# q and both gates of two blocks by Strassen's algorithm, in a stage of their own ahead of the mixers

## The chip, the cores and the metric

The kernel runs on one NeuronCore of a Trainium2 chip. The metric is the device time of one execution in microseconds (us). The core has five engines that run their own instruction streams in order and wait for one another by semaphores: TensorE (PE), VectorE (DVE), ScalarE (ACT), GpSimd (POOL) and SyncE (SP). Here SP only issues DMA transfers; POOL and ACT issue some as well. A static scheduler has fixed the order of the instructions on every engine before the program runs.

## The reference

One layer of a hybrid decoder in one inference step: 2048 prompt tokens (4 blocks of 512 for the kernel) and 32 sample tokens, width 1024, feed-forward width 4096.

```python
h = _rmsnorm(x, n1)
z = h @ w_in
hq, hf, hi, hg, sq, sk, sv, ga, gb = jnp.split(z, np.cumsum(IN_SPLITS)[:-1], axis=-1)
f = lb + (1.0 - lb) * jax.nn.sigmoid(hf)
o_hg, s_new = _hgrn_recurrence(heads(hq), heads(jnp.log(f)), heads(1.0 - f), heads(hi), s0, chunk)
y_a = (_rmsnorm(o_hg, hg_norm_w) * jax.nn.silu(hg)) @ w_up_a
y_b = o_b @ w_up_b                       # o_b: sliding-window attention of sq, sk, sv
m = jax.nn.sigmoid(ga) * y_a + jax.nn.sigmoid(gb) * y_b
x = x + m @ w_o
h2 = _rmsnorm(x, n2)
x = x + jnp.square(jax.nn.relu(h2 @ w_ff1)) @ w_ff2
```

hq has 512 columns, gb and ga have 1024 each. Everything is float32.

## The kernel before

**Precision.** A float32 operand is split into a high and a low part (`split_out`, L229: ACT rounds the high part with a cast, DVE subtracts it to get the low one). A product is then three matmuls into the same bank: high x high, high x low, low x high. So a product of 1024 rows by a tile of 128 columns and 512 tokens takes 8 x 3 = 24 matmuls of 512 columns.

**Order of the stages.** The loop over the blocks (L318) takes the four blocks b0 to b3 of 512 tokens; b3 carries the 32 sample tokens too (544 tokens, in two segments of 288 and 256 columns). A block goes through the mixers: hi (`colN512`, L391), four heads of hq (`colT`, L356), sq (`colN512`), skv (`colN`, L383), sliding-window attention (swa) with the heads of hf as filler, the levels of the HGRN recurrence (lv) with hg as filler, the outputs of the recurrence, then gate b, gate a, and W_o. After an odd block follows the MLP for the pair of blocks, f1 and f2, both by Strassen's algorithm (7 products for 8, classes Wpair and Unit, L971 and L1008) with the two blocks as halves of the token dimension. The pair b0, b1 has one chunk of 512 columns in it, the pair b2, b3 two of 264.

**The gates** (`gate`, L777): for each of 8 tiles j of 128 columns, 24 matmuls into a mm bank (gbb or gab in the trace: h times w_in), a tanh on ACT (sigmoid(x) = 0.5 tanh(x/2) + 0.5), 12 matmuls into a sw bank (ybb or yab: times W_up), and a DVE operation that joins them (L788). In gate a, POOL adds gate b's result pb (L813) and the sum is split into mT, W_o's operand. After every second j of the first two blocks, the program calls `w2_sums` (L302) once: 4 loads, 4 DVE sums, 4 stores that prepare the Strassen operands of W2 in DRAM.

**Operands and buffers.** The normalized, transposed input of a block lies split in SBUF (hT, two large slots of eight). It is made tile by tile (`load_T_parts`, L251): square on ACT, power on POOL (`rstd_of`, L197), scaling, 8 transposes on PE, products with the norm's weights on DVE, split. Block 0's tiles stand at the program's start, the tiles of b1 and b3 in W_o of the block before, those of b2 in f2 of the first pair (L1195). Weights are read in tiles of 128 x 1024 from a ring of 12 buffers (`wtile`, L73), loaded by SP and split (`split_w`, L148). The last operation of f2, in the first pair, is Fin (L1137): output rows are transposed back (fy), added to x (fx), squared, powered (fr) and scaled. The accumulators yacc of f2 lie in a pool that is freed after it.

Of the kernel before, what the change touches and what calls it, by code (L numbers as in the profile page):

```python
# [16 lines left out]
P = 128  # L17
# [26 lines left out]
def tile_hybrid_step(  # L44
# [188 lines left out]

    def geometry(bi):
# [16 lines left out]
    def load_T_parts(bi, i, hT, xt, on_dve=False, sm=None, junk=None, hwf=None):  # L251
        kind, r0, nr, c = geometry(bi)[5][i]
        src = xs if kind == "s" else xp[bi * bt + c * P:bi * bt + (c + 1) * P, :]
        N = f"ab{bi}{c}"
        x = []

        def pre():
            x.append(xt())
            nc.sync.dma_start(x[0][0:nr, :], src)
            norm_pre(x[0], x[0], nr, N, on_dve, sm, junk and junk())  # L260

        def out(half, tp, wb):
            hw = (hwf or t2)(f"hw_{N}_{half}")[:, 0:512].rearrange("p (k t) -> p k t", k=4)[:, :, 0:nr]
            nc.vector.tensor_tensor(hw, tp, wb, ALU.mult)
            split_out(hT[half][:, 0, :, r0:r0 + nr], hT[half][:, 1, :, r0:r0 + nr], hw)

        return pre, lambda: norm_post(x[0], nr, n1c, N, out)

    wk_ctx = ExitStack()
    wk = wk_ctx.enter_context(tc.tile_pool(name="wk0", bufs=1, reuse_waits="tile"))  # L270
    hT_next = start_T(0)
    x_first = op(6, F32, "x_first")
    for i in range(ncb):
        for part in load_T_parts(0, i, hT_next, lambda: x_first[:, i * D:(i + 1) * D], on_dve=True):
            part()
# [43 lines left out]
    for bi in range(nblk):  # L319
# [16 lines left out]
        hT_cur = hT_next  # L336
        h_acts = [(hT_cur[k // 4][:, 0, k % 4, :], hT_cur[k // 4][:, 1, k % 4, :]) for k in range(KD)]

        n4 = 4 * bt
        W0 = op(2, F32, "W0_" + B)  # L340
        W1 = op(3, F32, "W1_" + B)
        qW = W0[:, 0:n4].rearrange("p (h t) -> p h t", h=HH)
        kW = W0[:, n4:2 * n4].rearrange("p (h t) -> p h t", h=HH)
        fW = W1[:, 0:n4].rearrange("p (h t) -> p h t", h=HH)
        aW = W1[:, n4:2 * n4].rearrange("p (h t) -> p h t", h=HH)
        aflat = W1[:, n4:2 * n4]
# [6 lines left out]
        if smp:  # L353
            vS = wk.tile([NS, 512], F32, tag="vS", name="vS")
# [122 lines left out]
        while late:  # L477
            norm_post(*late.pop(0))
# [484 lines left out]
        with tc.tile_pool(name=f"f1_{sb}", bufs=1, reuse_waits="tile") as fp:  # L963
# [115 lines left out]
            for i, u in enumerate(units):  # L1079
                if i % len(chunks) == 0:  # L1080
                    u.pair.rest()
                if i >= ahead:
                    u.a()
# [262 lines left out]
```

## Time and profile before

| | |
|---|---|
| median of 3 runs | 2930.8 us (2928.26 to 2934.26) |
| the profiled execution | 2930.84 us |
| its span in the trace | 2929.1 us |
| mean granted TensorE clock | 0.992 |
| instructions of TensorE | 19967 matmuls and as many weight loads |
| bytes moved by DMA | 443.9 MB, mean 152 GB/s |

The page of the profile says for each engine how long it was busy and with how many instructions. A timeline row is a start, a duration, the engine, the line of the kernel, and the operation as out<-in. A windows row gives busy times by engine in a stretch of the span, with the granted clock and the DMA's share and rate. Stages of the first pair in the trace: the first transposes start at 10.6 us and hi at 18.2, gates b and a of block 0 run from 216 to 342, W_o to 390, block 1 to 758, f1 to 1078, f2 to 1399. The second pair ends at 2929.

### The profile page before, as it was taken

The numbers are of one execution on the slowest core, as the hardware profiler recorded it, in microseconds if no ns is written. First come the engines' busy times: TensorE is split into PE (matmuls) and PEld (weight loads), VectorE is DVE, ScalarE is ACT, GpSimd is POOL, SyncE is SP. The second block draws the span as 40 slices with busy tenths as digits, with TensorE's granted clock in tenths as the row PEclk, the third lists the DMA queues.
The fourth block names the chain that finished last, engine by engine and source line by source line (L and its number), as shares of the span: only waits on it lengthen the run. The fifth ranks groups of instructions, "written<-read, shape, count | busy, mean of one in ns | idle before, by whom it ended". The sixth has DMA issues, their size and how long they took to land.

```text
span 2929.1 us, 49035 instructions
## 1 busy us (share of the span) xinstructions
PE 2841.5 (97%) x19967; PEld 2453.5 (84%) x19967; DVE 1629.4 (56%) x2559; ACT 1136.1 (39%) x2093; POOL 215.0 (7%) x360
## 2 busy tenths in 40 slices
PE   7999999999899999999999999999998999999998
PEld 6778877788778888887777888878997999999998
DVE  5674434734777674454456343275347777754446
ACT  3443334423433344442354233333234333344433
POOL 0110111101200000000111011100003000000001
PEclk9999999999999999999999999999999999999999
DMA  7746342145654465565422434212346454485553
GB/s 251 238 154 219 105 144 66 45 122 158 197 165 155 159 232 206 196 214 173 151 64 68 125 115 135 62 52 84 116 133 197 151 157 140 146 304 179 186 195 104
DMA packets 410539, 443.92 MB, mean 152 GB/s; under 512 B 22588, under 2 KB 290840, under 8 KB 410296
## 3 DMA queue, kind: packets, MB, share of 16 engines
q1 hardware_dynamic: 402160, 413.48, 44.0%
q0 software_dynamic: 5600, 18.70, 2.1%
q10 hardware_dynamic: 2552, 8.60, 0.8%
q8 instruction: 157, 2.57, 0.4%
q14 instruction: 70, 0.57, 0.1%
HBM read 334.07 MB, written 107.64 MB: 151 GB/s over the span
## 4 chain that ended last, share of the span: by engine, by line
PE 43%; DMA 3%; DVE 2%; ACT 1%; issue 1%; POOL 1%; SPq 0%; POOLq 0%; DVEq 0%; ACTq 0%
PE f L1180 3%; PE f L1179 3%; PE f L1181 3%; PE fB L959 2%; PE fB L961 2%; PE fB L960 2%; PE gab L169 1%; PE gab L170 1%; PE gab L168 1%; PE gbb L170 1%; PE gbb L169 1%; PE gbb L168 1%; PE fD L959 1%; PE fD L961 1%; PE fD L960 1%
## 5 line engine op out<-in xcount | busy, mean ns | idle before, releaser
L1179 PE MATMUL f<-f2S,hw2T 128*128 128x264 f32 (+1 forms) x576 | 183.7, 319 | 0.0
L1180 PE MATMUL f<-f2S,hw2T 128*128 128x264 f32 (+1 forms) x576 | 183.6, 319 | 0.0
L1181 PE MATMUL f<-f2S,lw2T 128*128 128x264 f32 (+1 forms) x576 | 183.5, 319 | 0.0
L155 DVE TENSOR_TENSOR lw2T<-lw2T,hw2T 128x1024 fp32r<-128x1024 f32 x64 | 78.1, 1224 | 106.0 <-ACT hw2T L154 105.5
L959 PE MATMUL fB<-S,w1T 128*128 128x264 f32 (+1 forms) x384 | 124.2, 325 | 7.3 <-DVE c L1027 3.7
L1180 PE MATMUL f<-f2A,h_w2B 128*128 128x264 f32 (+1 forms) x384 | 122.5, 319 | 1.4 <-DVE f2A L155 1.4
L961 PE MATMUL fB<-S,w1T 128*128 128x264 f32 (+1 forms) x384 | 123.4, 322 | 0.0
L1179 PE MATMUL f<-f2A,h_w2B 128*128 128x264 f32 (+1 forms) x384 | 122.6, 319 | 0.8 <-ACT f2A L154 0.8
L960 PE MATMUL fB<-S,w1T 128*128 128x264 f32 (+1 forms) x384 | 123.3, 322 | 0.0
L1181 PE MATMUL f<-f2A,l_w2B 128*128 128x264 f32 (+1 forms) x384 | 122.2, 319 | 0.0
L154 ACT CAST hw2T<-lw2T 128x1024 fp32r<-128x1024 f32 x64 | 67.3, 1052 | 126.6 <-DMA lw2T<-w_T 114.3
L1180 PEld LDWEIGHTS f<-f2S,hw2T 128*128 128x128 f32 x576 | 108.4, 188 | 7.4
L1179 PEld LDWEIGHTS f<-f2S,hw2T 128*128 128x128 f32 x576 | 108.4, 188 | 7.4
L1181 PEld LDWEIGHTS f<-f2S,lw2T 128*128 128x128 f32 x576 | 108.0, 188 | 7.5
L169 PE MATMUL gbb<-hT_b,h_gbb 128*128 128x512 f32 (+2 forms) x320 | 113.2, 354 | 0.0
L168 PE MATMUL gbb<-hT_b,h_gbb 128*128 128x512 f32 (+2 forms) x320 | 113.1, 353 | 0.0
L170 PE MATMUL gbb<-hT_b,l_gbb 128*128 128x512 f32 (+2 forms) x320 | 112.9, 353 | 0.0
L169 PE MATMUL gab<-hT_b,h_gab 128*128 128x512 f32 (+2 forms) x320 | 111.7, 349 | 0.0
L170 PE MATMUL gab<-hT_b,l_gab 128*128 128x512 f32 (+2 forms) x320 | 111.6, 349 | 0.0
L168 PE MATMUL gab<-hT_b,h_gab 128*128 128x512 f32 (+2 forms) x320 | 111.4, 348 | 0.0
L155 DVE TENSOR_TENSOR f2S<-f2S 128x1024 fp32r<-128x1024 f32 (+1 forms) x64 | 79.4, 1242 | 51.9 <-ACT f2S L154 50.3
L231 DVE TENSOR_TENSOR l_w2B<-rw2B,h_w2B 128x1024 fp32r<-128x1024 f32 x48 | 58.8, 1225 | 81.1 <-ACT h_w2B L230 74.7
(717 smaller groups left out, 8821.1 us busy)
## 6 DMA issues: line engine op xcount, KB each, us to landing
w1r<-w_ff SPq DMA_DIRECT2D x150, 256.0 KB
lw2T<-w_T SPq DMA_DIRECT2D x64, 512.0 KB
rw2B<-w_ff SPq DMA_DIRECT2D x48, 512.0 KB
u_S<-s SPq DMA_DIRECT2D x128, 132.0 KB
f2S<-u_S SPq DMA_DIRECT2D x32, 528.0 KB
ws<-w_ff SPq DMA_DIRECT2D x64, 256.0 KB
r_gbb<-w_in SPq DMA_DIRECT2D x32, 512.0 KB
r_gab<-w_in SPq DMA_DIRECT2D x32, 512.0 KB
```

What stands on the lines that cost most here:

```text
L154: nc.scalar.copy(hi, F(lo))
L155: nc.vector.tensor_tensor(lo, F(lo), F(hi), ALU.subtract)
L168: nc.tensor.matmul(ps[:, 0:n], wh, rh, start=(k == 0), stop=False)
L169: nc.tensor.matmul(ps[:, 0:n], wh, rl, start=False, stop=False)
L170: nc.tensor.matmul(ps[:, 0:n], wl, rh, start=False, stop=(k == nk - 1))
L231: nc.vector.tensor_tensor(dl, src, F(dh), ALU.subtract)
L959: nc.tensor.matmul(ps, wh, ah, start=(first and k == 0), stop=False, skip_group_check=not first)
L960: nc.tensor.matmul(ps, wh, al, start=False, stop=False, skip_group_check=not first)
L961: nc.tensor.matmul(ps, wl, ah, start=False, stop=(last and k == 3), skip_group_check=not first)
L1179: nc.tensor.matmul(ps, wh, ah, start=first, stop=False, skip_group_check=cont)
L1180: nc.tensor.matmul(ps, wh, al, start=False, stop=False, skip_group_check=cont)
L1181: nc.tensor.matmul(ps, wl, ah, start=False, stop=lastk, skip_group_check=cont)
```

## The change

For each pair of blocks, a stage runs in front of the even block's mixers. It norms the tiles of both blocks. The even block's tiles are split into hT as before; all tiles are also stored to DRAM (hraw). skv and sq of the even block are computed and stored (zqk). Then the four quarters of the pair's input are read back in 16 loads on POOL's queue into a pool zq (14 buffers), and DVE makes the sums S1 to S4 and A22 that Strassen's algorithm needs. `strassen_T`, the code of f1 made general, computes q and both gates, 20 column tiles as 10 pairs with 7 products each. `z_fin` applies the tanh to gates, and stores q and gates to DRAM (zd). The mixers load qkv, q, and the tanh values (pb and ta) from there; gates only multiply by W_up, into sw and mm banks in turn. hi moves behind, as filler beside hf. The odd block's hT is read back from hraw in the even block's W_o and split there. The 16 sums of W2 are called in other places, eight for each block: in sq of b1, in both gates of b0 and b1, and in W_o of b0. For the second pair, the norm tiles of both blocks (nine, with the sample tile) are made during f2 of the first; the pool zq there follows f2's.

```diff
+        def out(half, tp, wb):
+            hw = x[1][:, half * 512:(half + 1) * 512].rearrange("p (k t) -> p k t", k=4)
+            nc.vector.tensor_tensor(hw[:, :, 0:nr], tp, wb, ALU.mult)
+            for (oo, s, n, d) in parts:
+                nc.gpsimd.dma_start(hraw[b][oo][...], hw[:, :, s:s + n])
+                if oo == 0:
+                    split_out(hT[half][:, 0, :, d:d + n], hT[half][:, 1, :, d:d + n], hw[:, :, s:s + n])
...
+            colN(C_SQ + 512, f"skv{B}", st_skv, step)
+            colN512(C_SQ, f"sq{B}", st_sq, lambda i: step())
+            while todo:
+                todo.pop(0)()
+            for k in range(4):
+                z = {n: zq.tile([P, Th], F32, tag="zs", bufs=14, name=f"z{n}{B}{k}") for n in ("a11", "a12", "a21", "a22", "s1", "s2")}
+                for n, o, g in (("a21", 1, 0), ("a22", 1, 1), ("a11", 0, 0), ("a12", 0, 1)):
+                    nc.gpsimd.dma_start(z[n], hraw[sb][o][(4 * g + k) * P:(4 * g + k + 1) * P, :])
+                tt(z["s1"], z["a21"], z["a22"], ALU.add)
+                tt(z["s2"], z["s1"], z["a11"], ALU.subtract)
+                tt(z["a21"], z["a11"], z["a21"], ALU.subtract)
+                tt(z["a12"], z["a12"], z["s2"], ALU.subtract)
+                for n, x in (("S2", "s2"), ("S1", "s1"), ("S3", "a21"), ("A22", "a22"), ("S4", "a12")):
+                    split_out(A[n][:, 0, k], A[n][:, 1, k], z[x])
+            zq_ctx.close()
...
+                strassen_T(f"z{sb}", NZ // 2, z_src, chunks, A, ..., z_fin, 6 if len(chunks) == 1 else 10)
...
-        colN512(C_HI, f"hi{B}", ev_v)
-        for h in range(HH):
-            colT(C_HQ, h, f"hq{B}{h}", ev_q)
...
+        nc.gpsimd.dma_start(qW, zd[bi][0:HH * P, ns:T].rearrange("(h p) t -> p h t", p=P))
...
-                ps = mm_ps("g" + N)
-                gemm_T(ps, n, [(gu[0][:, k, :], gu[1][:, k, :]) for k in range(KD)], h_acts, t0)
-                nc.scalar.activation(o, ps[:, 0:n], AF.Tanh, scale=0.5)
-                ps = sw_ps("y" + N)
+                ps = (sw_ps, mm_ps)[(j + i) % 2](f"y{z}{B}{j}_{t0}")
                 gemm_T(ps, n, [(uu[0][:, k, js], uu[1][:, k, js]) for k in range(4)], acts, t0)
```

In one chunk, a unit of `strassen_T` runs its first two products (A11 B11 into fB, A12 B21 into fC) six units ahead of the rest; with two chunks, ten ahead.

The following rows are the order of instructions, not times. VectorE at the start of the program: before, it works on hi's weights (l_hib is the low part of one) and on the tiles of block 0.

```order
L231 TENSOR_TENSOR l_hib_241<-r_hib_238,h_hib_240 128x1024
L264 TENSOR_TENSOR hw_ab_0_111<-tp_ab_0_106,n1c 128x512
L264 TENSOR_TENSOR hw_ab_1_120<-tp_ab_1_115,n1c 128x512
L216 TENSOR_SCALAR x_first<-x_first,rs_ab_154 128x1024
L231 TENSOR_TENSOR hT_b_95<-hw_ab_0_111,hT_b_95 128x4x128
```

After, behind the last tile of block 1 (hw_ab_428; za, zs, zS and zA are the quarters, sums and their split parts, l_sqb the low part of sq's weights):

```order
L410 TENSOR_TENSOR hw_ab_428<-tp_ab_1_443,n1c 128x512
L667 TENSOR_TENSOR zs1b_591<-za21b_589,za22b_590 128x512
L231 TENSOR_TENSOR zA_0_585<-za22b_590,zA_0_585 128x512
L668 TENSOR_TENSOR zs2b_592<-zs1b_591,za11b_587 128x512
L231 TENSOR_TENSOR l_sqb_457<-r_sqb_454,h_sqb_456 128x1024
L669 TENSOR_TENSOR za21b_589<-za11b_587,za21b_589 128x512
L670 TENSOR_TENSOR za12b_588<-za12b_588,zs2b_592 128x512
L231 TENSOR_TENSOR zS_0_583<-zs2b_592,zS_0_583 128x512
```

The first weight part of sq stands behind three operations on quarters that come back from DRAM.

VectorE after f2 of the first pair. Before, a weight of the next block's hi stands among Fin's operations:

```order
L1153 TENSOR_TENSOR nj_10921<-fy_384_1_11274,nj_10921 128x512
L231 TENSOR_TENSOR l_hib_11433<-r_hib_11430,h_hib_11432 128x1024
L1153 TENSOR_TENSOR fx_512_11289<-fy_512_1_11292,fx_512_11289 128x512
L1163 SCALAR_TENSOR_TENSOR nj_10921<-nj_10921,fr_384_11281,nfb_10922 128x512 x2
L1153 TENSOR_TENSOR fx_512_11289<-fy_512_0_11299,fx_512_11289 128x512
```

After, the sums and then sq's first weight follow Fin's last operations:

```order
L1298 TENSOR_TENSOR fx_896_11746<-fy_896_0_11756,fx_896_11746 128x512
L1308 SCALAR_TENSOR_TENSOR fx_768_11721<-fx_768_11721,fr_768_11738,nfb_11304 128x512 x2
L1308 SCALAR_TENSOR_TENSOR fx_896_11746<-fx_896_11746,fr_896_11763,nfb_11304 128x512 x2
L667 TENSOR_TENSOR zs1b_12036<-za21b_12034,za22b_12035 128x528
L231 TENSOR_TENSOR zA_1_12030<-za22b_12035,zA_1_12030 128x528
L668 TENSOR_TENSOR zs2b_12037<-zs1b_12036,za11b_12032 128x528
L669 TENSOR_TENSOR za21b_12034<-za11b_12032,za21b_12034 128x528
L231 TENSOR_TENSOR l_sqb_11902<-r_sqb_11899,h_sqb_11901 128x1024
```

sq's matmuls wait for the sums there too, through VectorE's order.

VectorE around the end of block 0 and the start of block 1, after (ws14t and ws15t begin a sum of W2, l_skvb is a weight of block 1's skv, h2w a tile of block 0 for the MLP):

```order
L468 TENSOR_TENSOR ws14t<-ws_6421,ws_6417 128x512
L231 TENSOR_TENSOR l_skvb_4543<-r_skvb_4540,h_skvb_4542 128x1024
L469 TENSOR_TENSOR ws_6417<-ws_6417,ws_6415 128x512
L231 TENSOR_TENSOR l_skvb_4549<-r_skvb_4546,h_skvb_4548 128x1024
L231 TENSOR_TENSOR l_hib_5007<-r_hib_5004,h_hib_5006 128x1024
L1104 TENSOR_TENSOR h2w_b_0_0_4481<-tp_fb_0_4476,cols 128x512
L468 TENSOR_TENSOR ws15t<-ws_6526,ws_6522 128x512
```

Before, at that place (W_o of block 0 and hq of block 1), no sum of W2 stands; the scheduler has put all 16 between the start of the program and block 0's gate a:

```order
L899 SCALAR_TENSOR_TENSOR y_b_3021<-wob_3_3268,y_b_3021 128x512
L231 TENSOR_TENSOR l_hqb_3623<-r_hqb_3620,h_hqb_3622 128x1024
L231 TENSOR_TENSOR l_hqb_3655<-r_hqb_3652,h_hqb_3654 128x1024
L231 TENSOR_TENSOR l_hqb_3687<-r_hqb_3684,h_hqb_3686 128x1024
L862 TENSOR_TENSOR h2w_b_0_0_3561<-tp_fb_0_3556,cols 128x512
```

So the 16 sums have moved from the stretch up to block 0's gate a into the stretch between block 0's attention and block 1's skv.

471 lines of the change are left out of this document (286 added, 185 removed).

## The prediction

> **What bounds the kernel now.** I read the page's totals first, then the windows view for where TensorE idles, then the timeline of PE for the cadence of its matmuls.
>
> ```profile
> span 2929.1 us, 49035 instructions
> PE 2841.5 (97%) x19967; PEld 2453.5 (84%) x19967; DVE 1629.4 (56%) x2559; ACT 1136.1 (39%) x2093; POOL 215.0 (7%) x360
> 0.00:20.00 20.00, 5.60 (x21) 4.83 (x22) 7.13 (x11) 9.22 (x15) 6.43 (x19) 1.00 0.85 292
> 20.00:44.00 24.00, 23.25 (x109) 18.71 (x108) 17.65 (x33) 8.23 (x14) 0.00 (x0) 1.00 0.63 203
> 26.00:66.00 40.00, 37.10 (x161) 29.49 (x160) 18.89 (x32) 13.22 (x19) 0.00 (x0) 1.00 0.84 276
> 44.20:68.90 24.70, 22.55 (x98) 18.05 (x97) 10.11 (x12) 7.08 (x10) 0.00 (x0) 1.00 0.78 261
> 758.00:790.00 32.00, 24.35 (x98) 19.01 (x97) 23.92 (x34) 16.75 (x25) 9.81 (x14) 0.89 0.83 268
> 790.00:870.00 80.00, 75.85 (x327) 61.48 (x326) 61.72 (x98) 26.72 (x50) 0.00 (x0) 0.98 0.51 166
> 1399.00:1420.00 21.00, 19.29 (x102) 15.11 (x101) 16.02 (x23) 10.08 (x23) 6.43 (x18) 1.00 0.51 176
> 2229.00:2265.00 36.00, 26.58 (x182) 25.67 (x181) 28.38 (x47) 16.02 (x27) 9.81 (x14) 0.86 0.75 240
> 2265.00:2300.00 35.00, 32.41 (x260) 31.59 (x259) 24.81 (x50) 13.21 (x30) 0.00 (x0) 1.00 0.52 159
> ```
>
> In a window's row stand its length, then the busy time of PE, PEld, DVE, ACT and POOL, the granted clock, the DMA share and GB/s. TensorE is busy 97% of the span, so the kernel is TensorE bound: a removed matmul is worth its cadence, and every us in which TensorE waits is lost. It waits in few places: the first 18 us, and the two starts of the MLP (758 and 2229), where a transposed, normalized operand must go through several engines and DRAM before the first product. Those stages are the nearest thing in this trace to the new one.
>
> ```profile
> 229.83 0.39 PE L170 MATMUL gbb<-hT_b,l_gbb 128*128 128x512 f32 x1
> 233.45 0.39 PE L168 MATMUL ybb<-ob_b,h_ubb 128*128 128x512 f32 x1
> 2061.58 0.30 PE L168 MATMUL gbb<-hT_b,h_gbb 128*128 128x288 f32 x1
> 2062.38 0.29 PE L168 MATMUL gbb<-hT_b,h_gbb 128*128 128x288 f32 x1
> 2060.15 0.28 PE L168 MATMUL ybb<-ob_b,h_ubb 128*128 128x256 f32 x1
> 2061.34 0.28 PE L169 MATMUL ybb<-ob_b,h_ubb 128*128 128x256 f32 x1
> 2319.78 0.28 PE L960 MATMUL fD<-S,w1T 128*128 128x264 f32 x1
> 2321.01 0.29 PE L961 MATMUL fB<-S,w1T 128*128 128x264 f32 x1
> ```
>
> A matmul's own 0.39 us overlaps the next one's; what counts is from start to start. The pairs lie 16, 6, 10 and 10 matmuls apart: 3.62/16 = 0.226 us for 512 columns, 0.133 for 288, 0.119 for 256 and 0.123 for 264.
>
> **1. The products: -50.** Before, each block computes 4 heads of q and 16 tiles of gates with 24 matmuls each: 480 a block. In the first pair that is 960 x 0.226 = 217.0 us, in the second 480 x 0.226 (block 2) + 480 x (0.133 + 0.119) (block 3, two segments) = 229.4 us. After, ten pairs of column tiles take 7 products of 12 matmuls: 840 x 0.226 = 189.8 us, and with two chunks of 264 columns 1680 x 0.123 = 206.6 us. Saved: 27.2 + 22.8 = 50.0 us. This is certain, since the gates run without gaps now. By the Trainium skill ("TensorE: Matmul & The Clock Gate", Back-to-back issue gap) a warm 512-column matmul alone takes N/2.4 + 2.5 ns, about 216 ns, where the trace has 226; by it the first pair would save 25.9 instead of 27.2 us, and the measurement decides.
>
> **2. The first front: +26 (18 to 36).** Before, q and the gates find their operand in SBUF. Now S1, S2, S3, S4 and A22 need block 1's normalized tiles, sent to DRAM and read back. Nothing hides this: at the program's start TensorE has only skv and 64 transposes.
>
> ```profile
> 10.60 1.97 PE L225 MATMUL tp_ab<-ident,x_first 128*128 128x128 f32 x8 [4.19 <-DVE x_first L216]
> 14.60 1.05 ACT L205 ACTIVATE junk<-x_first 128x1024 bf16<-128x1024 f32 x1
> 16.11 0.55 POOL L200 TENSOR_TENSOR rs_ab<-rs_ab,negh 128x1 f32<-128x1 f32 x1
> 18.23 0.78 PE L191 MATMUL ps_hib<-h_hib,hT_b 128*128 128x512 f32 x1
> h2T<-h2w_b POOLq DMA_DIRECT2D x16, 256.0 KB, 3.4
> S<-dS POOLq DMA_DIRECT2D x6, 512.0 KB, 4.9
> L231 DVE TENSOR_TENSOR l_gab<-r_gab,h_gab 128x1024 fp32r<-128x1024 f32 x8 | 9.8, 1225 | 17.8 <-ACT h_gab L230 15.5 <-PE gab L169 2.3
> L231 DVE TENSOR_TENSOR m_b<-ta_b,m_b 128x512 fp32r<-128x512 f32 x7 | 4.8, 689 | 8.3 <-ACT m_b L230 8.3
> ```
>
> Eight x tiles, two skv weights and the cache copies (some 6 MB) come first: at 292 GB/s (first window) skv's second weight is there near 20 us. skv is 96 x 0.119 = 11.4 us; with the transposes between it ends near 32. ACT has skv's last copy ahead of the last odd tile's square. So for that tile: square 1.05, power on POOL 0.75 (behind POOL's stores of the tile before, some 2), scaling 1.05, transposes 1, two DVE products of 0.69, near 40. The store lands 3.4 to 4.3 later, the reload 3.4 to 4.9 after that: 47 to 50. Then DVE does s1, A22's split and s2 (3 x 0.69) and only then the split of sq's first weight (1.23): TensorE's first full sq group comes at 51 to 54 on free queues. These are not free: 20 to 66 us carried 203 to 276 GB/s before, and the weights of sq and of six z pairs now ask for more. I take 56. By then TensorE has worked 11.4 + 7 us, so it idles some 37.5, against 14.4 + 0.75 in the first two windows before and some more behind them: 16. That is +21.5. From there DVE paces: an sq group has 6 x 0.69 + 1.23 = 5.4 us of splits and sums beside 24 x 0.226 = 5.4 of matmuls, and between the last sq group and the first z product 13 x 0.69 = 9 stand against 5.4, so +3.6, with +1 for waits inside: 26. Ends: landings of 3.4 give 18, doubled ones 36.
>
> **3. The second front: +16 (8 to 24).** Here sums wait behind the last rows of the MLP before it.
>
> ```profile
> 1398.67 1.04 PE L1151 MATMUL fy<-ident,yacc 128*128 128x128 f32 x8
> 1413.75 0.66 PE L1151 MATMUL fy<-ident,yacc 128*128 128x128 f32 x4 [0.42 <-DVE fx L1153]
> 1417.76 0.68 DVE L1153 TENSOR_TENSOR fx<-fy,fx 128x512 f32<-128x512 f32 x1
> 1418.53 0.63 ACT L205 ACTIVATE jkf<-fx 128x512 f32<-128x512 f32 x1 [3.21 <-DVE fx L1153]
> 1419.89 0.55 POOL L200 TENSOR_TENSOR fr<-fr,negh 128x1 f32<-128x1 f32 x1
> ```
>
> From the first transposes of the last output tiles to POOL's last power pass 21.8 us now, filled by hi's matmuls (TensorE busy 19.29 of 21). The reloads za stand on POOL's queue behind that power, and their buffers lie where yacc was. After the change DVE has fewer splits between, so I give the chain 17; two issues and a landing 5.5; s1, A22, s2, S3 and the weight's split 4.0: sq's first full group 26 to 27 after the start. Cover is skv, 11.4, and 40 transposes, 4.4: 16. Idle 10, less the 1.7 of now, +4 as DVE paces sq and the first z products as above, and +3.5 for the clock: the window 758:790 shows 0.89 granted over 32 us where 7.6 were idle, thus 3.5 lost. By the Trainium skill (same page, HAM clock gate) an idle window of about 3.4 us halves the clock until a busy one has passed; by it each front loses at most 1.7 to 3.4 us, which would move the sum by less than 2.
>
> **4. The stage itself: +5 (0 to 10).** strassen_T is f1's code. f1's first 80 and 35 us idle 4.15 and 2.6 with the operands there. Removed is hq's 2.15 of idle in its first run (44.20:68.90). Rest of the stage: a pair has 11 DVE operations on weights and 6 on results, 17 x 0.69 = 11.7 beside 19 us of matmuls.
>
> **5. Gates that only multiply by W_up: +5 (0 to 9).** A j now takes 12 x 0.226 = 2.7 us of TensorE instead of 8.1.
>
> ```profile
> 288.46 0.68 DVE L788 SCALAR_TENSOR_TENSOR ta_b<-ta_b,yab 128x512 f32<-128x512 f32 x1
> 289.22 1.30 POOL L813 TENSOR_TENSOR ta_b<-ta_b,pb_b 128x512 f32<-128x512 f32 x1 [66.54 <-DVE ta_b L788]
> 290.55 0.62 ACT L230 CAST m_b<-ta_b 128x512 fp32r<-128x512 f32 x1 [3.27 <-POOL ta_b L813]
> 291.20 0.69 DVE L231 TENSOR_TENSOR m_b<-ta_b,m_b 128x512 fp32r<-128x512 f32 x1 [2.06 <-ACT m_b L230]
> ```
>
> From product to split operand a j of gate a takes 3.43 us on four engines, and stages of one j overlap those of the next; W_o's first groups take k in order, 5.4 us each, and cover most. DVE's load in gate b of blocks 0 and 1 is the bound: eight j need 8 x 0.69, W_up's splits 4 x 1.23 (and gate a's early ones) and up to two sums of 4 x 0.69, near 17 against 21.7. A bank held too long costs 1 to 2 us a block.
>
> **6. The sums of W2: +5 (0 to 15).** All 16 stand between block 0's attention and block 1's skv. Each moves 2 MB; block 0's gates shrink from 126 to 43 us, so from its gates on seven to nine sums (18 MB) share some 115 us with 14 MB of weights and operands, near the 276 GB/s of 26:66. Sums 14 and 15 stand in DVE's order ahead of block 1's skv weight and h2w; were they 10 us late, TensorE would wait. Nothing in this trace shows it, so 0 and 15 are the ends.
>
> The attention stages (hi now beside hf, hg alone in the levels) I put at 0, within 5 a block: the same matmuls fill the same waits. Loads of q and of the tanh values are issued long before.
>
> **Sum.** -50 + 26 + 16 + 5 + 5 + 5 = +7; the profiled execution took 2930.84, the median too (2930.8), so **2938**.
>
> **Rivals.**
> - *Faster (0.28).* The two round trips are as short as their rows on a free queue, and DVE catches up: first front +17, second +9, the others 5 together: -50 + 31 = -19, 2912. For it: POOL's queue is separate and its landings are 3.4 to 4.9 in a loaded program as well. Against it: four engines and two hops in series, each with a queue ahead.
> - *Slower, by DMA (0.22).* If landings at the start double since 203 to 292 GB/s is already in flight, the first front is +36; the same limit makes the W2 sums late: +15. -50 + 36 + 16 + 5 + 5 + 15 = +27, 2958. It decides once a hop of hraw takes over 7 us. For it: shares of 0.84 at 26:66; against: later stages have 100 to 200 GB/s to spare.
> - *The reloads do not stand in the way (0.05).* If TensorE had sq at once and the sums went beside it, both fronts would shrink to some +5: -50 + 25 = 2906. DVE's order, with the sums ahead of sq's split, speaks against it.
>
> **How the numbers follow.** My forecast has 0.45, with ends of 2927 and 2948, as its terms miss independently. Range: 2908 to 2960, which leaves out the last rival and the tails. 0.2% is 5.9 us, about what a measurement here can tell from no change; 2925 to 2937 is "same". Of the forecast's 0.45, 0.02 lie below, 0.2 within and 0.23 above; the rivals add 0.28 (0.04 of it within) and 0.22 and 0.05. Faster 0.31, same 0.24, slower 0.45.
>
> **What would show it.** The window from 0 to the first sqb matmul shows 35 to 40 us of idle and DVE's zs1 waiting for za21; sq's first full group at 56 (50 says the faster rival, 63 the slower). After f2 of the first pair some 10 us of idle end with zs1's wait for a DMA. z's ten pairs take near 195 and 211 us. Gates of block 0 take near 45 us. If the stages of attention grow by more than 5 us a block, my zero there is wrong.

## The result, and the profile after

The changed kernel takes 2974.9 us (median of 4 runs, 2968.0 to 2976.3) where the kernel before takes 2932.5 beside it: a ratio of 1.0139 [1.0117, 1.0162], slower. The forecast was 2938 with a range of 2908 to 2960. The direction given the most chance was right; the size was not. Among the runs of one kernel the shorter ones show the higher granted clock (of the changed kernel, 2968.0 us at 0.983 and the others, 2974.7 to 2976.3, at 0.979 or 0.980), so one profiled run can lie some us off its median.

The page's totals of the changed kernel:

```profile
span 2974.5 us, 50416 instructions
PE 2822.1 (95%) x20087; PEld 2444.8 (82%) x20087; DVE 1772.7 (60%) x2877; ACT 1179.3 (40%) x2257; POOL 291.3 (10%) x485
```

TensorE falls from 97% to 95% of a longer span. Its matmul count rises (block 2's matmuls of 512 columns have become two of 264), so counts say little. I weigh them: each matmul at the median start-to-start time of its shape in the trace of before. That work falls from 2782.6 to 2728.3 us, by 54.3. The time not covered by it grows by 100, and 100 - 54 = 46 is the span's growth of 45.4.

The windows of the changed kernel show where (columns as in the prediction):

```profile
0.00:20.00 20.00, 7.33 (x27) 5.22 (x27) 8.22 (x14) 9.04 (x15) 9.97 (x23) 1.00 0.93 329
20.00:44.00 24.00, 18.56 (x124) 17.05 (x124) 10.63 (x24) 11.67 (x21) 8.28 (x14) 1.00 0.44 143
44.00:61.00 17.00, 2.59 (x14) 1.95 (x12) 4.17 (x7) 3.50 (x6) 9.20 (x16) 0.61 0.76 245
61.00:85.00 24.00, 23.95 (x97) 19.34 (x98) 24.00 (x37) 15.37 (x25) 3.23 (x6) 0.92 0.64 215
...
150.00:178.00 28.00, 22.80 (x100) 18.22 (x99) 12.92 (x20) 9.32 (x17) 0.00 (x0) 1.00 0.37 119
...
360.00:399.00 39.00, 35.93 (x853) 28.27 (x854) 30.82 (x63) 13.11 (x24) 0.00 (x0) 0.91 0.54 170
...
461.00:507.00 46.00, 43.31 (x192) 35.51 (x190) 23.32 (x31) 10.09 (x11) 4.01 (x3) 1.00 0.79 267
507.00:564.00 57.00, 43.21 (x225) 37.93 (x224) 27.61 (x36) 18.97 (x26) 14.30 (x25) 0.85 0.81 269
564.00:641.00 77.00, 77.00 (x407) 54.08 (x405) 43.28 (x79) 35.89 (x113) 9.55 (x18) 1.00 0.33 100
...
1459.00:1472.00 13.00, 0.23 (x1) 0.24 (x2) 4.32 (x7) 2.83 (x5) 6.46 (x13) 0.57 0.96 329
1472.00:1479.00 7.00, 7.00 (x19) 5.32 (x20) 7.00 (x11) 4.06 (x7) 1.07 (x2) 0.58 0.77 280
```

The two fronts are the rows 44:61 and 1459:1472: TensorE stands still while DMA and DVE prepare the sums. A third hole was not forecast: 507:564, the start of block 1, where TensorE works 43.2 of 57 us at a granted clock of 0.85 and the DMA carries 269 GB/s.

The waits of TensorE in the changed kernel (total us, times, longest):

```profile
PE ps_sqb L191 <- ACT h_sqb L230: 23.3, 2, 12.9
PE wob L191 <- DVE ta_b L1023: 10.0, 4, 2.7
PE tp_fb L225 <- DVE h2w_b L1104: 8.8, 3, 5.9
PE fB_z L238 <- ACT c_z L299: 6.9, 4, 3.3
...
PE ps_sqb L191 <- DVE y_b L1141: 5.9, 1, 5.9
```

The first row is the two fronts. The second is one wait in each block: the second bank of W_o still holds a product of gate a that VectorE has not read. The third and the last are mostly block 1's start.

### The profile page after: what moved, and what is told of

The parts are those of the page before. It is cut to its first block, busy times and chain, and to the rows that moved or that the text cites. A ratio compares the mean times of both kernels' runs of the same rounds, so it can differ in the third digit from the quotient of the medians.

```text
span 2974.5 us, 50416 instructions
## 1 busy us (share of the span) xinstructions
PE 2822.1 (95%) x20087; PEld 2444.8 (82%) x20087; DVE 1772.7 (60%) x2877; ACT 1179.3 (40%) x2257; POOL 291.3 (10%) x485
## 5 line engine op out<-in xcount | busy, mean ns | idle before, releaser
L238 PE MATMUL fB_f<-S,w1T_f 128*128 128x264 f32 (+1 forms) x384 | 123.9, 323 | 6.0 <-DVE c_f L301 3.8
L240 PE MATMUL fB_f<-S,w1T_f 128*128 128x264 f32 (+1 forms) x384 | 123.0, 321 | 0.0
L239 PE MATMUL fB_f<-S,w1T_f 128*128 128x264 f32 (+1 forms) x384 | 122.9, 320 | 0.0
L230 ACT CAST w1T_f<-w1r_f 128x512 fp32r<-128x512 f32 x128 | 76.4, 620 | 62.2 <-DVE w1r_f L275 29.5
L231 DVE TENSOR_TENSOR w1T_f<-w1r_f,w1T_f 128x512 fp32r<-128x512 f32 x128 | 85.9, 687 | 21.8 <-ACT w1T_f L230 21.4
L231 DVE TENSOR_TENSOR w1B_f<-w1r_f,w1B_f 128x512 fp32r<-128x512 f32 x96 | 65.4, 687 | 39.4 <-ACT w1B_f L230 38.5
L299 ACT COPY c_f<-fB_f 128x264 f32<-128x264 f32 (+1 forms) x80 | 36.0, 450 | 133.0 <-PE fB_f L240 130.3
L154 ACT CAST f2S<-f2S 128x1024 fp32r<-128x1024 f32 (+1 forms) x64 | 67.9, 1064 | 51.0 <-DMA f2S<-u_S 48.5
L191 PE MATMUL wob<-h_wob,m_b 128*128 128x512 f32 x192 | 76.6, 399 | 10.0 <-DVE ta_b L1023 10.0
```

The source lines that it names most:

```text
L154: nc.scalar.copy(hi, F(lo))
L191: nc.tensor.matmul(ps[0:nr], lh, uh[:, kk, :], start=(k == 0), stop=False)
L230: nc.scalar.copy(dh, src)
L231: nc.vector.tensor_tensor(dl, src, F(dh), ALU.subtract)
L238: nc.tensor.matmul(ps, wh, ah, start=(first and k == 0), stop=False, skip_group_check=not first)
L239: nc.tensor.matmul(ps, wh, al, start=False, stop=False, skip_group_check=not first)
```

## The experiments

All times are medians of 4 runs, with the ratio to the kernel before on the same chip. The changed kernel's 2974.9 is the base for differences; a difference under some 10 us lies within the intervals' overlap, and is then read from the trace.

### The sums of W2

**1. Without the sums, first try.** f2 reads a copy of a quarter of W2 in place of T1 to T4; no sums are made.

```diff
-    def w2_sums(i):
...
+                    nc.gpsimd.dma_start(wT1[i * P:(i + 1) * P, :], w2[i * P:(i + 1) * P, 0:512])
```

> Left out: the 16 sums of W2 with their loads, waits and stores. f2 of both pairs finds in place of T1 to T4 a plain copy of W2's first quarter (4 MB, made during f1 of the first pair on POOL's queue), so the matmuls and the loads of f2 are as in the changed kernel. Theory (the sums are what was lost between W_o of block 0 and block 1's skv): that stretch, 103 us from the start of W_o to the end of skv in the changed kernel, shrinks to 83 to 87, the gates and W_o of block 0 hardly move, and the time is 2950 to 2957 (18 to 25 below the changed kernel). Rival (the sums only fill time that block 1's start loses anyway, by its own weights and h2w): the stretch stays above 97 and the time is 2965 to 2975. The prediction's term for the sums was +5, with 0 and 15 as ends; by it 2970 with ends of 2975 and 2960.

2964.8, ratio 1.0125 [1.0095, 1.0156]. From the start of W_o (475) to the end of skv (560) it takes 85 us in place of 104, as the theory said. But the copies have nothing to wait for and run at the program's start: skv's first low part comes at 31.4 us (25.1 in the changed kernel), z starts 2 us later and lasts 9 longer, and so hi starts 11 us later. The total decides nothing; the next run mends that.

**2. Without the sums, copies held back to f1.**

```diff
+                    nc.gpsimd.dma_start(wT1[i * P:(i + 1) * P, :], F(A22)[:, 0, i % 4, 0:512])
```

> Left out: the 16 sums of W2 again, but nothing is added at the program's start: f2 reads in place of T1 to T4 a 4 MB array that f1 of the first pair writes from A22's high part (16 stores of 256 KB on POOL's queue), which can't start before f1. Theory (the sums cost 18 us at block 1's start, and the run without them before this one lost 11 of it again because its plain copies ran on POOL's queue and the DMA at the program's start): first full group of sq at 60 to 62, z from 84 to 86, W_o of block 0 to skv's end 83 to 87 us in place of 103, the time 2951 to 2959. Rival (what the sums cost comes back behind them, in the attention or f1): the stretch is short and the time is 2963 to 2972.

2965.8 (2958.4 to 2973.4), ratio 1.0117 [1.0094, 1.0140]. The profiled execution took 2958.4. Its windows:

```profile
460.00:506.00 46.00, 43.69 (x193) 35.83 (x193) 19.87 (x23) 13.63 (x17) 4.97 (x7) 1.00 0.49 161
506.00:548.00 42.00, 39.29 (x228) 34.74 (x227) 13.39 (x15) 15.36 (x22) 13.55 (x25) 0.96 0.46 144
```

The same matmuls that took 57 us take 42, at 144 in place of 269 GB/s; W_o's start to skv's end is 88 us, 15.5 less, and the first front is as it was (z starts at 86.0). So the hole at block 1's start is the sums' own. In the total it is 9 by the median, with intervals that overlap, and 18 by the profiled run. So the loss is shown at its place; how much of it reaches the total is not.

**3. Where the changed kernel loses it.** SyncE, VectorE and TensorE at that place, in the changed kernel's timeline (start, duration, idle before and its cause; a q marks an issue; L144 loads a weight, L473 stores a sum):

```profile
496.13 1.77 SPq L473 DMA_DIRECT2D w_T<-ws  x3
498.00 0.40 SPq L144 DMA_DIRECT2D r_sqb<-w_in  x1
506.77 1.23 DVE L231 TENSOR_TENSOR l_sqb<-r_sqb,h_sqb 128x1024 fp32r<-128x1024 f32 x1 [8.07 <-ACT h_sqb L230]
512.43 2.48 DVE L1141 SCALAR_TENSOR_TENSOR y_b<-wob,y_b 128x512 f32<-128x512 f32 x4
513.26 0.76 PE L191 MATMUL ps_sqb<-h_sqb,hT_b 128*128 128x512 f32 x1 [5.90 <-DVE y_b L1141]
...
522.78 0.69 DVE L468 TENSOR_TENSOR ws13t<-ws,ws 128x512 f32<-128x512 f32 x1 [7.88 <-DMA ws<-w_ff]
533.63 0.69 DVE L468 TENSOR_TENSOR ws14t<-ws,ws 128x512 f32<-128x512 f32 x1 [7.98 <-DMA ws<-w_ff]
534.25 1.22 DVE L231 TENSOR_TENSOR l_skvb<-r_skvb,h_skvb 128x1024 fp32r<-128x1024 f32 x1
...
537.95 0.40 SPq L144 DMA_DIRECT2D r_hib<-w_in  x1
544.20 1.23 DVE L231 TENSOR_TENSOR l_hib<-r_hib,h_hib 128x1024 fp32r<-128x1024 f32 x1 [5.55 <-ACT h_hib L230]
545.34 1.28 DVE L1104 TENSOR_TENSOR h2w_b<-tp_fb,cols 128x512 f32<-128x512 f32 x2
```

VectorE stands 7.9 us for the loads of one sum and 8.0 for the next, and behind the second in its order is skv's weight. But TensorE has sq to work on meanwhile, and skv's first product starts at 538.5, right behind sq and a transposition. TensorE's two long waits there, 5.9 us each, come by another way. SyncE issues weights and sums in one order, and the stores of a sum wait there for VectorE: the third weight of sq is issued at 498.0, behind three such stores, where run 2 issues it at 489.8, and ScalarE can cast it only at 505.7. On VectorE its low part and the four operations of sum 12 stand ahead of the reading of W_o's product (y_b) that frees sq's first bank. The second wait (up to 546.1, the 5.9 in the row of tp_fb above) is the same with hi's first weight, issued at 537.95 (516.8 in run 2), ahead of h2w. This is read from the trace: no run gave the sums' transfers another queue and left the sums in their place.

**4. Block 1's eight sums behind its skv weights.**

```diff
-            colN512(C_SQ, f"sq{B}", ev_sq, lambda i: sum_next() if i % 2 else None)
+            colN512(C_SQ, f"sq{B}", ev_sq)
...
+            with tc.issue_after(splits_w[-1][1].ins):
+                for _ in range(8):
+                    sum_next()
```

> One edit: block 1's eight sums of W2 are issued on DVE only behind block 1's skv weights, so that they lie beside its attention and gates (564 to 716, 101 GB/s in the first half) instead of beside W_o of block 0 and sq and skv of block 1 (267 GB/s). My theory: the 23 us lost from 461 to 564 come from these sums, on the DMA queues and in DVE's order; they fall to 5 or less, the time by 15 to 20 us, to 2955 to 2960. Rival: that stretch waits for the reload of block 1's hT or for its weights anyway, or the sums are as much in the way later; less than 6 us, 2969 or more.

2972.9, ratio 1.0151 [1.0133, 1.0169]. skv ends at 546.6 instead of 564.3, and then:

```profile
547.00:633.00 86.00, 80.12 (x401) 55.51 (x399) 57.83 (x102) 35.51 (x112) 11.60 (x20) 0.96 0.73 235
633.00:675.00 42.00, 36.08 (x867) 28.44 (x866) 28.76 (x59) 14.43 (x26) 0.00 (x0) 0.92 0.28 69
```

The sliding-window stage takes 86 us in place of 77 and the levels 42 in place of 34. The hole has moved with the sums.

**5. The sums on GpSimd.**

```diff
-        tt = nc.vector.tensor_tensor
+        tt = nc.gpsimd.tensor_tensor
```

> One edit: the 64 additions of the W2 sums run on POOL instead of DVE; loads, stores and their places stay about as they were. Putting half of the sums later gained 19 us from 461 to 564 and lost 17 in block 1's attention, so the sums cost wherever they lie. My theory: what costs is DVE's order: a sum that waits for its loads (19.3 us in six waits in the trace) holds up the attention, W_o and weight operations queued behind it; with the sums on POOL 12 to 20 us of the 2975 go, 2955 to 2963. Rival: what costs is their 32 MB on the DMA queues and SP's order; then the time stays within 5 us of 2975, or rises, since POOL's own queue (rotary, reads of q and qkv, h2T stores) now waits behind sums.

3012.4, ratio 1.0296 [1.0268, 1.0325], 37 worse. One row of its windows, block 0's levels:

```profile
373.00:423.00 50.00, 40.49 (x867) 31.09 (x866) 42.05 (x62) 15.08 (x28) 18.42 (x12) 0.83 0.60 182
```

The same levels took 39 us (360:399). GpSimd's queue has the rotary embedding and the gates' additions, and they now stand behind sums that wait for loads. The loads and stores themselves stayed on SyncE's queue.

**6. The sums in f1 of the first pair**, first in three tiles of the weight ring, then in four tiles of their own.

```diff
+        r0, r1, t3 = wtile(F32, f"ws{i}0"), wtile(F32, f"ws{i}1"), wtile(F32, f"ws{i}t")
+        nc.gpsimd.dma_start(r0, w2[i * P:(i + 1) * P, :])
...
-                       f1_fin, 6 if len(chunks) == 1 else 10)
+                       f1_fin, 6 if len(chunks) == 1 else 10, w2_sums if sb == 0 else None)
```

> The same 16 sums, one after each of the 16 units of f1 of the first pair, in three tiles of the weight ring, loads and stores on POOL's queue. Theory (the sums hurt by where they stand: beside a stage with much DMA and few matmuls; f1 has 20 us of matmuls a unit and 100 to 160 GB/s): f1 grows by under 6 us from 322, the stretch at block 1's start falls to 83 to 87, the time is 2950 to 2960. Rival (three of twelve ring tiles and 2.8 us of VectorE a unit make f1 wait for weights): f1 grows by over 15 us and the time stays at 2968 to 2985.

3004.5, ratio 1.0255 [1.0218, 1.0291]: the rival. Block 1's start gains 14 us and f1 loses 31. The second form has z with four units ahead and W_o's banks changed as well (below), and in f1 four units ahead and 12 result tiles:

```diff
+                        r[kh, nh] = fp.tile([P, 512], F32, tag="ws", bufs=4, name=f"ws{i}{kh}{nh}")
...
-                       f1_fin, 6 if len(chunks) == 1 else 10)
+                       f1_fin, 4 if len(chunks) == 1 else 10, w2_sums if sb == 0 else None)
```

> Four units ahead in z and in f1 of the first pair, W_o's first groups in the hg banks, and the sums of W2 in f1 of the first pair in four tiles of their own (f1 has 12 result tiles in place of 16 for that), so that the weight ring is left alone. In the ring they made f1 31 longer. Theory (f1 grew by the three ring tiles): f1 grows by at most 10, the stretch at block 1's start falls to 85 to 90, the time is 2945 to 2958. Rival (f1 grew by the transfers: 187 GB/s became 252, and its weights came late): f1 grows by 15 to 30 again, and the time is 2962 to 2985.

2977.4, ratio 1.0151 [1.0130, 1.0171], 20 above the same kernel with the sums left in place. W_o's start to skv's end is 84 us, as the theory said, but f1 takes 354 in place of 319. Its windows:

```profile
765.00:900.00 135.00, 117.87 (x491) 93.53 (x490) 106.59 (x167) 49.23 (x83) 39.12 (x68) 0.96 0.81 267
900.00:1000.00 100.00, 85.25 (x346) 68.68 (x345) 70.95 (x116) 27.18 (x49) 27.64 (x51) 0.91 0.78 255
```

**7. The same sizes of f1 without the sums**, to tell transfers from fewer tiles:

```diff
-                       lambda ln, name: fp.tile([P, ln], F32, tag="st", bufs=16 * len(chunks), name=name),
-                       f1_fin, 6 if len(chunks) == 1 else 10)
+                       lambda ln, name: fp.tile([P, ln], F32, tag="st", bufs=12 if sb == 0 else 16 * len(chunks), name=name),
+                       f1_fin, 4 if len(chunks) == 1 else 10)
```

> As the kernel with four units ahead in z and W_o's first groups in the hg banks (2957.66), and in f1 of the first pair four units ahead and 12 result tiles, without any sum moved. It splits the 35 us by which f1 grew when the sums were put there with these same sizes. Theory (the transfers did it): f1, 319 us, stays within 8, and the time is 2955 to 2968. Rival (the fewer tiles did it, since a result's tile comes free only when its store has landed): f1 grows by 20 or more, and the time is 2976 to 2992.

2957.6, ratio 1.0084 [1.0052, 1.0116]. f1 takes 314 us from its first product to f2's, against 319 with 16 tiles, and its windows read:

```profile
780.00:900.00 120.00, 111.58 (x473) 89.48 (x472) 95.12 (x148) 50.47 (x84) 9.81 (x14) 0.97 0.57 189
900.00:1000.00 100.00, 100.00 (x443) 82.81 (x442) 68.42 (x109) 35.59 (x63) 0.00 (x0) 1.00 0.46 154
```

The fewer tiles cost nothing; the sums with their transfers did it, 40 us against this run, at 255 to 267 GB/s in place of 154 to 189. With them VectorE stood 41 us for the sums' loads and stores, ScalarE 104 us for VectorE's operations on the weights (13 without the sums) and 46 us for the loads of weights (4 without).

**8. Block 1's eight sums in z of the first pair**, where the DMA has the most room.

```diff
+                            r[kh, nh] = zp.tile([P, 512], F32, tag="ws", bufs=4, name=f"ws{i}{kh}{nh}")
+                            nc.gpsimd.dma_start(r[kh, nh], w2[(kh * NP + i) * P:(kh * NP + i + 1) * P, nh * 512:(nh + 1) * 512])
...
-                           z_fin, 4 if len(chunks) == 1 else 10)
+                           z_fin, 4 if len(chunks) == 1 else 10, z_sum if sb == 0 else None)
```

> As the kernel with four units ahead in z and W_o's first groups in the hg banks (2957.66), with block 1's eight sums of W2 moved into z of the first pair: four tiles of their own, 12 result tiles of z in place of 16, transfers on POOL's queue; block 0's eight stay. Theory (a sum is free where the DMA has room: z carried 119 to 158 GB/s, and eight sums are 16 MB over 186 us, 90 GB/s more, against 250 where f1 suffered): z lasts at most 192, from W_o of block 0 to the end of block 1's skv 84 to 90 us in place of 104, the time 2940 to 2950. Rival (z is as near to its limit as f1 was): z grows by 12 or more, and the time is 2952 to 2975.

2963.7, ratio 1.0111 [1.0087, 1.0134]: the rival again. Block 1's start falls to 83 us, a gain of 21, and z grows from 186 to 208.5:

```profile
85.00:150.00 65.00, 58.87 (x253) 46.48 (x251) 45.05 (x71) 22.47 (x41) 22.63 (x42) 1.00 0.88 291
150.00:178.00 28.00, 24.25 (x95) 19.85 (x96) 15.66 (x26) 9.68 (x17) 9.11 (x17) 0.88 0.76 250
178.00:275.00 97.00, 90.55 (x389) 74.38 (x389) 49.60 (x74) 38.76 (x67) 5.48 (x11) 0.96 0.39 131
```

The transfers were not spread over z: 291 GB/s were moved in the first 65 us. My 90 GB/s more was a mean that the queue did not keep. VectorE stood 24 us in z for the sums' loads, and TensorE 12.2 us for copies on ScalarE (5.2 in the changed kernel). z's 12 result tiles in place of 16 were not tried alone; in f1 they cost nothing.

### The banks of W_o

**9. W_o's first groups in the hg banks**, which no gate uses.

```diff
-            rings = (sw_ps, sw_ps, hg_ps, hg_ps, mm_ps)
+            rings = (hg_ps, hg_ps, sw_ps, sw_ps, mm_ps)
...
-                rings = ((sw_ps, sw_ps, hg_ps, hg_ps), (mm_ps, mm_ps, sw_ps, sw_ps))[cg]
+                rings = ((hg_ps, hg_ps, sw_ps, sw_ps), (mm_ps, mm_ps, hg_ps, hg_ps))[cg]
```

> One edit: W_o's first groups take the hg banks instead of the sw banks. W_o waited 10.0 us in all, four times, for DVE's operation that empties the last yab bank. My theory: that wait is for the bank alone; it goes, and the time falls by 5 to 10 us, to 2965 to 2970. Rival: W_o also needs the last operand tiles of gate a, whose chain lags; the wait moves into W_o and the time stays within 4 us of 2975.

2965.5, ratio 1.0118 [1.0098, 1.0139], 9.4 less. TensorE's waits there begin:

```profile
PE ps_sqb L191 <- ACT h_sqb L230: 23.9, 2, 13.3
PE tp_fb L225 <- DVE h2w_b L1104: 8.9, 3, 6.0
PE tp_fb L225 <- ACT h_b L218: 8.4, 3, 3.8
```

The row of wob with its 10.0 us is gone, and the time fell by about that.

### The first front and z

**10. sq's weights ahead of the sums S.**

```diff
+                with tc.issue_after(sqw[-1][0].ins), tc.issue_after(sqw[-1][1].ins):
+                    tt(z["s1"], z["a21"], z["a22"], ALU.add)
...
```

> One edit: in both front stages, ACT and DVE do all four weight splits of sq ahead of the sums of the quarters (an order of issue, no work added or removed). My theory: TensorE's waits in the two fronts (39.8 us not worked up to 84.8, 20.5 us from 1440 to 1497) are made by that order alone, since sq needs nothing of the sums and the first 33 us of the z stage need only hT; then sq starts near 45 us instead of 61 and right behind skv in the second front, and the time falls by 20 to 35 us, to 2940 to 2955. Rival: the read-back of the tiles is what is late, and the waits only move from sq to the first products of z; then the time stays within 8 us of 2975.

2986.8, ratio 1.0196 [1.0181, 1.0212], 12 worse. sq starts at 50.9 instead of 61.0 and z at 77.2 instead of 84.8, but z then lasts 203 us instead of 192:

```profile
51.00:77.00 26.00, 24.94 (x97) 19.85 (x96) 16.70 (x25) 9.59 (x16) 10.10 (x18) 0.85 0.85 272
77.00:190.00 113.00, 102.88 (x422) 82.68 (x421) 65.00 (x101) 45.09 (x81) 4.33 (x8) 0.94 0.44 138
```

From 77.5 to 89.6 us VectorE works the sums S without a break, halves of z's weights stand behind them, and TensorE waits 3.5 us for such halves. Most of the rest of z's 11 us is the clock, 0.94 over these 113 us where it was 1.00. By z's end 3 of the 12 us are lost; the others lie in later stages and were not taken apart.

**11. hi of the even blocks in the front**, as cover, kept in DRAM.

```diff
+            colN512(C_HI, f"hi{B}", st_hi, lambda i: step())
...
-        colN512(C_HI, f"hi{B}", ev_v)
+        if odd:
+            colN512(C_HI, f"hi{B}", ev_v)
```

> One edit: the even blocks' hi (96 matmuls, 21.8 us) is computed in the front stage ahead of skv and sq, kept in DRAM and read back, instead of beside the attention. My theory: the fronts' 40 and 20 us without work are waits for the chain norm, DRAM, sums with nothing to cover them; hi covers 15 to 22 us in each, and attention had no need of it as a filler (before, hf alone filled it with no loss). So 25 to 40 us go: 2935 to 2950. Rival: as with sq put first, what TensorE gains at the start of z is lost in it, since z is paced by its weights and sums, and attention lacks the filler: less than 10 us, 2965 or more.

2992.8, ratio 1.0221 [1.0203, 1.0240], 18 worse. The front's hole only moves:

```profile
57.00:69.00 12.00, 11.87 (x100) 11.67 (x98) 1.57 (x4) 1.70 (x5) 6.31 (x11) 1.00 0.81 266
69.00:78.00 9.00, 0.00 (x0) 0.00 (x0) 9.00 (x16) 6.32 (x12) 3.76 (x7) 0.69 0.97 361
```

hi covers the wait for the transfers, which ends at 68.8 us. Then VectorE works 16 operations of the sums without a break, and the cast of sq's first weight, loaded long before, stands behind them at 77.3; TensorE waits 9.5 us for it. So the second row is the order of the sums ahead of sq's weights, and hi in front together with run 10's order was not tried. z ends 21 us later, 298.4 for 277.2, and block 0's gates end when they did (463 for 460.9): what hi cost in front, the attention saves, though block 0's levels take 49 us instead of 39. Block 1's attention takes 88 instead of 77, and block 1 ends 14 us late. Block 2 loses more, with its levels at 50 instead of 39.

**12. z with four units ahead in place of six.**

```diff
-                           z_fin, 6 if len(chunks) == 1 else 10)
+                           z_fin, 4 if len(chunks) == 1 else 10)
```

> z of the first pair runs the first two products of four units ahead in place of six, so that the ring of twelve weight tiles holds fewer halves of weights that are not yet used up. Theory (z's waits at 149 to 178 us come from the full ring): z of the first pair falls from 192 to 187 to 189 us, the time to 2969 to 2972. Rival (z waits for the loads themselves and for copies behind casts on ScalarE, and fewer units ahead leave less cover while the sums S are made): z's length stays at 191 or more or its start moves later, and the time is 2975 to 2982.

2965.5, ratio 1.0128 [1.0100, 1.0155]. z lasts 186 us in place of 192: its wait at 149 to 178 us is gone, as the theory of the full ring has it. The total is 4 below what was expected.

### Together

**13. Runs 4, 9 and 10 together; 9 and 11 with the sums on GpSimd; 6 with 9.**

> The three edits together. If they act in stretches of their own as I think, their gains add up: the sum of the three within 8 us, by my numbers 2975 - 27 - 8 - 18 = 2922, about the kernel before. If they share one limit (DMA), the gain is clearly less than their sum.

2965.9, ratio 1.0126 [1.0107, 1.0145]. Far above: what runs 4 and 10 gain at first is waited away behind it, only the banks' 9 us stay.

> hi in front, the hg banks first for W_o, and the sums of W2 on POOL together. If the three act apart, the gains add: 2975 less 9 (measured for the banks) less 32 less 16, so 2918, under the kernel before (2930). If they share a limit, 2935 or more.

3003.8, ratio 1.0259 [1.0233, 1.0284]: the same, with the cost of GpSimd's queue.

> The sums in f1 of the first pair, as in the run before it in this list, and W_o's first groups in the hg banks. If the two gains are separate places they add: 9 below the kernel with the sums in f1 alone, so 2941 to 2951 by the theory there. If they are the same wait seen twice, 0 to 4 below it. Not faster than the kernel before in either case, since both fronts and z's waits stay (some 52 us against 54 of saved matmuls, with 10 more in the attention and f2).

2992.7, ratio 1.0215 [1.0181, 1.0248], 12 below the kernel with the sums in f1's ring: the banks' gain adds, by the medians; the rest fell with run 6.

**14. Runs 9 and 12 together**, the best that was found:

> z of the first pair with four units ahead, and W_o's first groups in the hg banks. Theory (the two waits lie in different stages and add): 5 + 9 = 14 below the changed kernel, 2957 to 2964. Rival (block 1's start and the first front set where the time goes, and what is won before them waits there again): 2964 to 2970.

2957.7, ratio 1.0084 [1.0070, 1.0098], clear of the changed kernel's interval. 17.2 less, against 9.4 + 9.4 apart: the two add. z's window:

```profile
150.00:178.00 28.00, 28.00 (x125) 23.21 (x124) 13.84 (x21) 12.96 (x23) 0.00 (x0) 1.00 0.38 121
```

TensorE is busy throughout where it was busy 22.8 of 28. The kernel is still 27 us slower than the one before.

**15. That, with sq's weights ahead of the sums S.**

> As the run before it in this list, and the splits of sq's four weights ahead of the sums S on ScalarE and VectorE. With six units ahead that order had z start 8 us earlier and last 11 longer, by full ring and late weights. Theory (the ring was what took it back): with four ahead z starts at 77 to 79 and lasts at most 192, and the time is 3 to 8 below the run before it. Rival (the sums S stand behind sq's weights then, and z's first full unit waits for them whatever the ring): z ends no earlier than in that run, and the time is the same or up to 12 above it.

2962.6, ratio 1.0106 [1.0092, 1.0120], 5 above run 14. In the first pair z starts at 75.5 and lasts 193, so 2.6 us remain of the 10 by which it starts earlier; in the second pair z lasts 213 instead of 206 and uses up the lead that was left. So the full ring was not what took run 10's gain, or not alone.

## Why the prediction was wrong

The terms, in us, against what the two traces show (loss after minus loss before in each stage, by the weighing above):

| term | forecast | measured |
|---|---|---|
| 1 products | -50 | -54 |
| 2 first front | +26 (18 to 36) | +23 |
| 3 second front | +16 (8 to 24) | +17 |
| 4 the stage itself | +5 (0 to 10) | +12 |
| 5 gates that only multiply by W_up | +5 (0 to 9) | +11 |
| 6 sums of W2 | +5 (0 to 15) | +20 |
| attention | 0 | +9 |
| f1 and f2 of the first pair, not forecast | 0 | +8 |
| sum | +7 | +46 |

The miss is 39 us. The sums of W2 are the largest part with 15, then the attention with 9, f1 and f2 with 8, the stage with 7 and the gates with 6; terms 1 to 3 give 6 back. Run 2 without any sums still takes 2966 us, so no single term explains it.

**1 to 3 held,** 2 and 3 in part by luck. The first front ran as it was followed, only later on each hop. From the changed kernel's timeline:

```profile
50.93 1.54 POOL L412 DMA_DIRECT2D hraw<-hw_ab  x2 [3.45 <-DVE hw_ab L410]
54.94 0.56 POOL L666 DMA_DIRECT2D za21b<-hraw  x1 [2.48 <-DMA hraw<-hw_ab]
59.50 0.69 DVE L667 TENSOR_TENSOR zs1b<-za21b,za22b 128x512 f32<-128x512 f32 x1 [8.08 <-DMA za22b<-hraw]
61.05 1.65 PE L191 MATMUL ps_sqb<-h_sqb,hT 128*128 128x512 f32 x3 [10.36 <-ACT h_sqb L230]
```

The last tile was stored at 51 where "near 40" was forecast: on ScalarE the squares of the last tiles stood behind the copies of skv's results (a wait of 6.4 us up to 32.7), and on POOL the power behind stores. The reload was issued at 54.9, the last quarter for s1 and A22 landed near 59.4, and sq's full groups began at 61 instead of 56. That cost 5 us, but sq then ran 96 matmuls in 24 us, 2 lost where 3.6 and 1 were put on top for VectorE, and the first stretches worked more: errors that offset each other. The rival of long hops (over 7 us) did not decide: the issue of the reload waited 2.5 us and its landing took some 4. In the second front 13 idle us and 2.9 lost to the clock (7 us at 0.58) stand against 10 and 3.5; the 4 for VectorE's pace did not come, but 3 more us were idle ahead of the hole (from 1440 to 1459). By the Trainium skill ("TensorE: Matmul & The Clock Gate", HAM clock gate) a halved clock lasts until a busy window of about 3.4 us has passed, from which I estimate at most 3.4 us lost for a front; the trace's 2.9 agrees with it.

**6 failed, and is the largest part of the miss.** The step "sums 14 and 15 stand in DVE's order ahead of block 1's skv weight and h2w; were they 10 us late, TensorE would wait" named the place, and the 15 of its rival was near the price. It was given 5 because "seven to nine sums (18 MB) share some 115 us" came near a rate (276 GB/s) that TensorE had stood at 26 to 66 us. The rate did not tell the waits. Sums 13 and 14 came 8 us late on VectorE, and TensorE did not wait for skv's weight behind them; what the step left out is SyncE's order, in which the weights of sq and hi stand behind stores that wait for the sums (run 3). The runs show the cost: run 2 takes 15.5 us out of that place with the sums, run 8 takes 21 by moving eight of them, and wherever the sums went they cost as much or more (17 in block 1's attention, 22 in z, 31 to 40 in f1). The bound of 15 was too low too: with the waits and a clock of 0.85 the place lost 20.

**5 had the wrong cover.** The gates lost nothing, W_o lost 11. From the changed kernel's timeline, the end of block 2's gate a:

```profile
1888.84 0.39 PE L170 MATMUL yab<-oa_b,l_uab 128*128 128x512 f32 x1
1891.55 0.69 DVE L231 TENSOR_TENSOR m_b<-ta_b,m_b 128x512 fp32r<-128x512 f32 x1 [1.83 <-ACT m_b L230]
1892.16 0.68 DVE L1023 SCALAR_TENSOR_TENSOR ta_b<-ta_b,yab 128x512 f32<-128x512 f32 x1
1892.89 0.50 PE L191 MATMUL wob<-h_wob,m_b 128*128 128x512 f32 x1 [2.31 <-DVE ta_b L1023]
```

A j of gate a takes VectorE 3.3 to 4.3 us with its waits for ScalarE, and TensorE now 2.7, so that the readings of yab fall behind the products: this one comes 3.3 us after the last product was issued, and it isn't yet the last reading. "W_o's first groups take k in order, 5.4 us each, and cover most" looked at the operand mT alone. W_o's second bank is one that gate a has written, and stands before that cover begins. In the kernel before, TensorE needed 8.1 us a j and nothing fell behind. Run 9 gives W_o's first groups other banks and takes the wait away.

**4 was sized from f1**, whose ring has the same six units ahead. z's first units come while its operands are still being made, so that six units' halves filled the ring (run 12: 6 us of the 7 lost in z of the first pair). The other pair's z lost 7 too, and the table takes off 2 that hq of block 1 lost before. TensorE is busy 204 of 206 us in that z, so most of its 7 is cadence: by the median of the trace before a product of 264 columns weighs 0.121 us where the prediction took 0.123 from ten. Over 1680 of them that moves 3.4 us between terms 1 and 4, and is most of the 4 by which term 1 came out larger.

**Attention and f2.** The zero was right within 5 for block 0 (+4) and block 3 (-5, about), not for block 2 (+10). f2 of the first pair, with nine norm tiles in it where four stood, lost 6 more than before, and f1 2. The tiles in f2 were a part of the change that the sum had no term for. None of these was taken apart by a run, so their cause stays open.

**The rivals.** Slower by DMA had the right size for the sums of W2, but its sign, a hop of hraw of over 7 us in the first front, did not show, and it stopped at 2958. Nothing speaks for the two faster ones.

## What to carry to other kernels

When a long stage is cut short, look at what used to run beneath it: here 16 sums with 32 MB of transfers had cost little under the work from 27 to 258 us, and cost 15 to 40 us in each place that they had after the change. Price such moved background work by the wait of what is queued right behind it, on the engine that computes and on the one that issues its transfers, not by a stage's mean rate. When a producer gets faster, check which banks the next stage writes first, not only the operands that it reads.

## What the runs showed of the hardware

A stage's mean DMA rate said little of whether TensorE waits: 267 to 269 GB/s at block 1's start, 255 to 267 in f1 and 291 in z came with lost time, while in the kernel before 276 (26 to 66 us) came with 2.9 us of idle in 40, and 361 (run 11, 69 to 78 us) was reached for a short stretch. By the Trainium skill ("DMA: Bandwidth & Descriptors", Specifications) a core's share of the memory's rate is about 358 GB/s; the 361 over 9 us lies close to it, and the time was lost at rates well below it.

A load issued behind stores that wait for another engine starts late: at block 1's start SyncE issued a weight of sq 8 us and one of hi 21 us later than without the sums (run 3). That is not all that a sum costs, since in f1 and z the sums' transfers were on POOL's queue and time was lost there too. How much the transfers and how much the order on VectorE bound in those stages was not told apart.
